# A decoder trunk's head: squares summed by TensorE, nine-column sums for the conditioning, another chain to h, constant products

## The chip, the core and the metric

The kernel runs on one core of a Trainium2 chip. The metric is the device time of one execution in microseconds; the kernel before has a median of 1943.88 (1943.31 to 1947.8 over three runs). Engines have names: TensorE (PE, with its weight loads PEld), VectorE (DVE), ScalarE (ACT), GpSimd (POOL) and SyncE (SP). SyncE and GpSimd issue the DMAs that matter here, each on a queue of its own.

## The reference

One layer of a decoder trunk, for 256 prompt tokens and 8 sequences of 8 sample tokens, 320 tokens in all, of width 2048. Nine conditioning vectors (one of the prompt, eight of the samples) give six modulations of width 2048, and the first two make h:

```
mod = silu(c) @ w_ada + b_ada                      # (9, 6 * 2048)
sh1, sc1, g1, sh2, sc2, g2 = split(mod, 6)
h = rmsnorm(x, norm1_g) * (1 + sc1) + sh1
p = h @ w_in                                       # q, k, v, og, u, ga, gb, alr
o = gated linear attention(q, k, v, alr);  y_b = pooling(u)
x = x + g1 * ((sigmoid(ga) * norm(o) * silu(og) + sigmoid(gb) * y_b) @ w_o)
h2 = rmsnorm(x, norm2_g) * (1 + sc2) + sh2
x = x + g2 * ((silu(h2 @ w_gate) * (h2 @ w_up)) @ w_down)
```

All is fp32. Weights are read once from HBM.

## The kernel before

Activations lie transposed, 128 channels by 320 tokens a tile, 16 tiles for a width of 2048 (KT). A product with fp32 accuracy is made of three fast ones (`mm3`, L177 to L179): the weight is split by ScalarE into a high part (`whi`, L162) and by VectorE into a low part (`wlo`, L163), the activation in the same way (`hh`, `hl`), and low times low is left out. The weights of `w_in` come in by SyncE (`raw`, L218 and L154), three buffers of 512 KB and four of each split part.

**The head** is what the change touches. It makes h while the first group's projections run. The width of h is cut into slices of 2, 2, 2, 2, 4 and 4 tiles; each slice goes through all eleven column blocks ("units") of the first head group, in six groups, and the sums are collected in SBUF. A slice needs its h tiles only, so the conditioning of later tiles runs as background work between the units (`bg`).

Conditioning: for two tiles of h there are two blocks, section 0 (shift) and section 1 (scale), 2 MB of `w_ada` each. `hada_load` brings a block into one of two buffers (tag `araw`); the first two blocks come by SyncE behind `xt`, the others by GpSimd, each as soon as the block two before it has been multiplied. `hada` multiplies it with silu(c) in 16 products, four at a time side by side in the array (L241), which leaves four partial sums of nine rows each, 32 partitions apart. ScalarE copies them to SBUF (`adasb`, L244), TensorE transposes them (L133), VectorE adds the four (L249), then the bias (L252) and for the scale 1 and the norm's weight (L254). The later sections go the same way through `ada_burst` (L306).

h itself: squares by ScalarE (L529), added up to one tile by VectorE (L531 to L533), summed over the channels by one product with ones (L535), root and reciprocal (L537, L538), x times that (`h_pre`, L544), then `h_post`: the affine step (L347 to L349) and the split into `hh` and `hl` (L342, L343).

The order of the work on each engine is made once, when the kernel is built, by a scheduler that goes by priority and by its own idea of times; on the chip every engine takes its list strictly in order, and each SyncE or GpSimd DMA waits in its list too. `high_priority` moves work ahead, `issue_after` forbids it to stand ahead of a given instruction.

Of the kernel before, what the change touches and what calls it, by code (L numbers as in the profile page):

```python
# [11 lines left out]
F32 = mybir.dt.float32  # L12
# [7 lines left out]
P = 128  # L20
# [57 lines left out]
def body(tc, A):  # L78
# [52 lines left out]
    def tr(out, in_):  # L131
        k = in_.shape[0]
        PE.transpose(out, in_, ident[:k, :k])  # L133

    identr = cp.tile([P, P], F32R, name="identr")

    def trr(out, in_):
# [95 lines left out]
    def hada(sec, b0, t, pool):  # L233

        blk = sec * KT + b0
        w = 2 * P
        ps = misc()
        with tc.high_priority():
            for r in (3, 2, 1, 0):
                for j in range(4):  # L240
                    PE.matmul(ps[32 * j:32 * j + 32, 0:w], lhsT=scT[:, 4 * r + j, :], rhs=t[:, 4 * r + j, :],  # L241
                              start=r == 3, stop=r == 0, tile_position=(0, 32 * j))
        sb = pool.tile([P, w], F32, tag="adasb", name=nm("adasb"))
        S.copy(sb, ps[:, 0:w])  # L244
        pt = misc()
        for i in range(2):
            tr(pt[:, i * P:(i + 1) * P], sb[:, i * P:(i + 1) * P])
        dst = mod[:, blk:blk + 2, :]
        V.tensor_reduce(dst, pt[:, 0:w].rearrange("p (b j r) -> p b r j", b=2, j=4)[:, :, 0:9, :],  # L249
                        axis=AX.X, op=ALU.add)  # L250
        bb = bada[:, blk:blk + 2].unsqueeze(2).broadcast_to([P, 2, 9])
        V.tensor_tensor(dst, dst, bb, op=ALU.add)  # L252
        if sec == 1:
            V.scalar_tensor_tensor(dst, dst, 1.0, N1G[:, b0:b0 + 2].unsqueeze(2).broadcast_to([P, 2, 9]),  # L254
                                   op0=ALU.add, op1=ALU.mult)

# [21 lines left out]
    def anchor(src):  # L278

        return G.tensor_copy(tick, src).ins  # L280
# [12 lines left out]
    def ada_burst():  # L293
# [18 lines left out]
        for q in range(0, nb, 2):  # L312
            wq = min(2, nb) * P
            sb = apool[0].tile([P, wq], F32, tag="adasb", name=nm("adasb"))
            S.copy(sb, ps[:, q * P:q * P + wq])
# [3 lines left out]
        V.tensor_reduce(mod[:, blk:blk + nb, :], pt[:, 0:w].rearrange("p (b j r) -> p b r j", b=nb, j=4)[:, :, 0:9, :],  # L319
                        axis=AX.X, op=ALU.add)  # L320
# [20 lines left out]
    def hilo(hi, lo, x):  # L341
        S.copy(hi, x)  # L342
        V.tensor_sub(lo, x, hi.bitcast(F32))  # L343
# [166 lines left out]
    with tc.tile_pool(name="head", bufs=1) as xp:  # L510
# [7 lines left out]
            nc.sync.dma_start(xt[:, k:k + 4], A["xt"][:, k:k + 4])  # L518
        raws = {(s, 0): hada_load(s, 0, xp, nc.sync) for s in (0, 1)}
        make_identity(nc, ident)  # L520
        S.copy(identr, ident)
        csig = xp.tile([P, KT, 9], F32, name="csig")
        S.activation(csig, c9, AF.Sigmoid)
        V.tensor_tensor(scT[:, :, 0:9], c9, csig, op=ALU.mult)

        ssq = xp.tile([P, 4, T], F32, name="ssq")
        for k in range(0, KT, 4):
            sq = xp.tile([P, 4, T], F32, tag="sqx", name=nm("sqx")) if k else ssq
            S.activation(sq, xt[:, k:k + 4], AF.Square)  # L529
            if k:  # L530
                V.tensor_tensor(ssq, ssq, sq, op=ALU.add)  # L531
        V.tensor_tensor(ssq[:, 0:2], ssq[:, 0:2], ssq[:, 2:4], op=ALU.add)
        V.tensor_tensor(ssq[:, 0], ssq[:, 0], ssq[:, 1], op=ALU.add)  # L533
        prs = misc()
        PE.matmul(prs[:, 0:T], lhsT=ones, rhs=ssq[:, 0], start=True, stop=True)  # L535
# [29 lines left out]

        g0 = new_group(0)
        new_gates(g0)
        def h_rows(b):

            def load(s):  # L570
                with tc.issue_after(landed) if (s, b) == (0, 2) else nullcontext():
                    raws[s, b] = hada_load(s, b, xp, nc.gpsimd)
            return ([lambda: load(0), lambda: (h_pre(b), h_pre(b + 1)), lambda: load(1),
                     lambda: hada(0, b, raws.pop((0, b)), xp),
                     lambda: (hada(1, b, raws.pop((1, b)), xp), h_post(b), h_post(b + 1))])

        landed = anchor(raws[0, 0][:, KT - 1, 0:1])
        for f in h_rows(0)[1::2]:
            f()
        with tc.high_priority():  # L580
            h_rows(0)[4]()
        us = [units(0)[0:2], units(0)[4:5], units(0)[2:4]] + [units(0)[n:n + 2] for n in (5, 7, 9)]
        apool = [xp]
        for si, (k0, k1) in enumerate(SLICES):
# [9 lines left out]
                    nc.gpsimd.dma_start(invc, A["cf"][:, 0:64])  # L594
            done = 0
            for ui, pair in enumerate(us):
                want = len(bg) * (ui + 1) // len(us)
                while done < want:
# [562 lines left out]
```

## Time and profile before

| | us |
|---|---|
| median of three runs | 1943.88 |
| the profiled execution | 1946.53 |
| its span, first to last instruction | 1944.8 |
| TensorE busy | 1894.2 (97%) |
| first product of the projections starts at | 29.42 |
| granted clock of TensorE, mean | 0.994 |

The page gives busy time by engine; the timeline gives single instructions in order of time, with the idle time before them and what ended it in brackets. "x2" merges neighbours of one kind, with the time from the first start to the last end. The records of a plain fp32 product come in two passes, those of a transpose and of the fast products in one.

### The profile page before, as it was taken

To read this page: it belongs to the slowest core of one execution; us is meant where nothing else is said; L and a number is where in the kernel's file an instruction comes from. 1 tells how busy PE (TensorE), PEld (TensorE's weight loads), DVE (VectorE), ACT (ScalarE), POOL (GpSimd) and SP (SyncE) were. 2 spreads that over 40 slices of the span, in tenths; PEclk is the share of its full clock that TensorE was granted. 3 is DMA by queue.
4 is the path that set the end of the run, shared out by engine and by line. 5 is a ranking of instruction groups with operands and counts; after the bars stand their busy time and mean duration, and the time that the engine had idled before them with its cause. 6 is when DMAs were issued, how large, how long until landed. Compare 5 with 4: busy or idle time off the path is not lost.

```text
span 1944.8 us, 34340 instructions
## 1 busy us (share of the span) xinstructions
PE 1894.2 (97%) x13698; PEld 1795.0 (92%) x13698; DVE 1019.5 (52%) x1977; ACT 806.4 (41%) x1441; POOL 151.5 (8%) x292
## 2 busy tenths in 40 slices
PE   5999999999999999999999999999999999999996
PEld 4888898988998899889989999999999999999996
DVE  4775564656355646555574444444444444444454
ACT  4333454544354453444453333343333343434442
POOL 1110111121011102101020000000000000000000
PEclk9999999999999999999999999999999999999998
DMA  9996566677766767588644555445554444444542
GB/s 352 365 354 217 194 221 227 210 254 264 247 242 211 262 240 282 192 290 313 208 164 151 185 184 186 143 144 153 146 156 151 149 151 152 152 149 145 153 146 92
DMA packets 102464, 398.54 MB, mean 205 GB/s; under 512 B 12084, under 2 KB 14576, under 8 KB 90008
## 3 DMA queue, kind: packets, MB, share of 16 engines
q1 hardware_dynamic: 77616, 261.73, 42.3%
q0 software_dynamic: 24400, 134.54, 18.0%
q8 instruction: 107, 1.75, 0.4%
q14 instruction: 53, 0.43, 0.1%
q10 hardware_dynamic: 288, 0.08, 0.0%
HBM read 374.48 MB, written 22.05 MB: 204 GB/s over the span
## 4 chain that ended last, share of the span: by engine, by line
PE 87%; DMA 2%; DVE 1%; issue 0%; POOL 0%; ACT 0%; DVEq 0%; POOLq 0%; ACTq 0%
PE ps L177 26%; PE ps L178 26%; PE ps L179 26%; PE pm L306 3%; DMA araw<-w_ada 2%; PE pm L133 1%; PE pm L846 1%; PE pm L808 1%; PE pm L797 0%; DVE yg L1112 0%; PE pm L873 0%; PE pm L651 0%; PE pm L559 0%; DVE S L878 0%; PE pm L745 0%
## 5 line engine op out<-in xcount | busy, mean ns | idle before, releaser
L163 DVE TENSOR_TENSOR wlo<-raw,whi 128x512 fp32r<-128x512 f32 x952 | 660.9, 697 | 764.2 <-ACT whi L162 745.8
L162 ACT CAST whi<-raw 128x512 fp32r<-128x512 f32 x952 | 589.2, 621 | 954.5 <-PE ps L178 888.8
L177 PE MATMUL ps<-hh,whi 128*128 128x320 f32 x1408 | 442.7, 315 | 4.2 <-ACT hh L342 2.9
L179 PE MATMUL ps<-hh,wlo 128*128 128x320 f32 x1408 | 439.3, 312 | 2.3 <-DVE wlo L163 2.3
L178 PE MATMUL ps<-hl,whi 128*128 128x320 f32 x1408 | 440.1, 313 | 0.0
L178 PE MATMUL ps<-h2l,whi 128*128 128x320 f32 x1408 | 435.2, 309 | 0.0
L177 PE MATMUL ps<-h2h,whi 128*128 128x320 f32 x1408 | 435.2, 309 | 0.0
L179 PE MATMUL ps<-h2h,wlo 128*128 128x320 f32 x1408 | 434.7, 309 | 0.0
L177 PEld LDWEIGHTS ps<-hh,whi 128*128 128x128 f32 x1408 | 265.7, 189 | 17.8 <-issue 9.9
L178 PEld LDWEIGHTS ps<-hl,whi 128*128 128x128 f32 x1408 | 265.9, 189 | 9.3 <-issue 8.8
L179 PEld LDWEIGHTS ps<-hh,wlo 128*128 128x128 f32 x1408 | 265.8, 189 | 7.9 <-issue 4.8
L177 PEld LDWEIGHTS ps<-h2h,whi 128*128 128x128 f32 x1408 | 264.5, 188 | 3.4 <-ACT ah L342 3.4
L178 PEld LDWEIGHTS ps<-h2l,whi 128*128 128x128 f32 x1408 | 264.7, 188 | 0.1
L179 PEld LDWEIGHTS ps<-h2h,wlo 128*128 128x128 f32 x1408 | 264.6, 188 | 0.0
L177 PE MATMUL ps<-ah,whi 128*128 128x320 f32 x704 | 217.8, 309 | 0.0
L179 PE MATMUL ps<-ah,wlo 128*128 128x320 f32 x704 | 217.5, 309 | 0.0
L178 PE MATMUL ps<-al,whi 128*128 128x320 f32 x704 | 217.5, 309 | 0.0
L178 PEld LDWEIGHTS ps<-al,whi 128*128 128x128 f32 x704 | 132.3, 188 | 0.1
L177 PEld LDWEIGHTS ps<-ah,whi 128*128 128x128 f32 x704 | 132.3, 188 | 0.1
L179 PEld LDWEIGHTS ps<-ah,wlo 128*128 128x128 f32 x704 | 132.3, 188 | 0.0
L177 PE MATMUL ps<-mh,whi 128*128 128x320 f32 x256 | 79.2, 309 | 0.2 <-DVE mg L505 0.2
L178 PE MATMUL ps<-ml,whi 128*128 128x320 f32 x256 | 79.2, 309 | 0.0
(271 smaller groups left out, 1455.4 us busy)
## 6 DMA issues: line engine op xcount, KB each, us to landing
raw<-w_gu SPq DMA_DIRECT2D x176, 512.0 KB, 3.9
raw<-w_in SPq DMA_DIRECT2D x154, 512.0 KB, 4.6
araw<-w_ada POOLq DMA_DIRECT2D x64, 1024.0 KB, 9.2
raw<-w_down SPq DMA_DIRECT2D x80, 512.0 KB, 3.6
hraw<-w_ada POOLq DMA_DIRECT2D x28, 1024.0 KB, 8.9
S<-state_gla POOLq DMA_DIRECT2D x16, 1024.0 KB, 8.2
o_gs<-S POOLq DMA_DIRECT2D x16, 1024.0 KB, 8.4
raw<-w_o SPq DMA_DIRECT2D x32, 512.0 KB, 5.9
```

The costliest lines, as they stand in the source:

```text
L133: PE.transpose(out, in_, ident[:k, :k])
L162: S.copy(hi, raw)
L163: V.tensor_sub(lo, raw, hi.bitcast(F32))
L177: PE.matmul(ps, lhsT=whi, rhs=xhi, start=start, stop=False)
L178: PE.matmul(ps, lhsT=whi, rhs=xlo, start=False, stop=False)
L179: last_mm[:] = [PE.matmul(ps, lhsT=wlo, rhs=xhi, start=False, stop=stop).ins]
L306: PE.matmul(ps[32 * j:32 * j + 32, 0:w], lhsT=scT[:, k0 + r + j, :], rhs=ada_raw[n][:, r + j, :], start=k0 == 0 and first, stop=k0 + nk == ...
L808: PE.matmul(pt, lhsT=E["kdn"][:, s, d * P:(d + 1) * P], rhs=E["vn"][:, s], start=s == 0, stop=s == 1)
L846: PE.matmul(pt[32 * j:32 * j + 32, :], lhsT=qeP[:, d, 4 * gg + j, :], rhs=E["S0", gg, d][:, j], start=False, stop=d == 0, tile_position=(0 ...
```

## The change

Five things, all but one in the head.

The squares: each quarter of x is squared into a buffer of its own (two of them), VectorE adds its halves, and TensorE sums the two tiles that are left with two products each, eight in all, into one accumulator.

The nine-column sums: in place of two transposes and VectorE's reduction, each half of `adasb` is the stationary operand of a product with `sel`, a 128 by 9 matrix of zeros and ones, which adds the four partial sums and turns them in one. VectorE then adds the bias while it reads the result. This goes for all six sections.

The chain to h: `h_post` is written out. ScalarE makes the high part of the prompt's tokens straight from x, scale and shift; VectorE does the samples, then the same affine step for the low part.

The order: a block's products may no longer stand ahead of the last `mm3` recorded before them, the copies and sums have high priority, and the background work has three steps a row in place of five, dealt out one unit group earlier. The next load of a buffer is recorded right behind the product that frees it; the anchor on the first block's landing (`tick`) is gone.

The constant products: `busy` issues products of ones that nobody reads, two behind the first block's sums and three behind the second's.

```diff
+    sel = cp.tile([P, 9], F32, name="sel")
+    bada1 = cp.tile([P, KT], F32, name="bada1")
...
-        with tc.high_priority():
+        with tc.high_priority(), tc.issue_after(last_mm[0]) if last_mm else nullcontext():
...
-        for i in range(2):
-            tr(pt[:, i * P:(i + 1) * P], sb[:, i * P:(i + 1) * P])
-        dst = mod[:, blk:blk + 2, :]
-        V.tensor_reduce(dst, pt[:, 0:w].rearrange("p (b j r) -> p b r j", b=2, j=4)[:, :, 0:9, :],
-                        axis=AX.X, op=ALU.add)
-        bb = bada[:, blk:blk + 2].unsqueeze(2).broadcast_to([P, 2, 9])
-        V.tensor_tensor(dst, dst, bb, op=ALU.add)
-        if sec == 1:
-            V.scalar_tensor_tensor(dst, dst, 1.0, N1G[:, b0:b0 + 2].unsqueeze(2).broadcast_to([P, 2, 9]),
-                                   op0=ALU.add, op1=ALU.mult)
+        with tc.high_priority():
+            sb = pool.tile([P, w], F32, tag="adasb", name=nm("adasb"))
+            S.copy(sb, ps[:, 0:w])
+            pt = misc()
+            for i in range(2):
+                mm = PE.matmul(pt[:, 16 * i:16 * i + 9], lhsT=sb[:, i * P:(i + 1) * P], rhs=sel, start=True, stop=True)
+            for i in range(2):
+                if sec == 1:
+                    V.tensor_scalar(mod[:, blk + i, :], pt[:, 16 * i:16 * i + 9], bada1[:, b0 + i:b0 + i + 1],
+                                    N1G[:, b0 + i:b0 + i + 1], op0=ALU.add, op1=ALU.mult)
+                else:
+                    V.tensor_scalar(mod[:, blk + i, :], pt[:, 16 * i:16 * i + 9], bada[:, blk + i:blk + i + 1], None,
+                                    op0=ALU.add)
+        return mm.ins
...
-                tr(pt[:, (q + i) * P:(q + i + 1) * P], sb[:, i * P:(i + 1) * P])
+                PE.matmul(pt[:, 16 * (q + i):16 * (q + i) + 9], lhsT=sb[:, i * P:(i + 1) * P], rhs=sel, start=True, stop=True)
...
-        ssq = xp.tile([P, 4, T], F32, name="ssq")
+        prs = misc()
         for k in range(0, KT, 4):
-            sq = xp.tile([P, 4, T], F32, tag="sqx", name=nm("sqx")) if k else ssq
+            sq = xp.tile([P, 4, T], F32, tag="sqx", bufs=2, name=nm("sqx"))
             S.activation(sq, xt[:, k:k + 4], AF.Square)
-            if k:
-                V.tensor_tensor(ssq, ssq, sq, op=ALU.add)
...
-        PE.matmul(prs[:, 0:T], lhsT=ones, rhs=ssq[:, 0], start=True, stop=True)
+            V.tensor_tensor(sq[:, 0:2], sq[:, 0:2], sq[:, 2:4], op=ALU.add)
+            for j in range(2):
+                PE.matmul(prs[:, 0:T], lhsT=ones, rhs=sq[:, j], start=k + j == 0, stop=k + j == KT - 3)
...
         def h_post(k):
+
             xh = xhs.pop(k)
-            affine(xh, 1, 0, k)
-            hilo(hh[k], hl[k], xh)
+            V.tensor_tensor(s3(xh[:, TP:T]), s3(xh[:, TP:T]), mods(1, k), op=ALU.mult)
+            S.activation(hh[k][:, 0:TP], xh[:, 0:TP], AF.Identity, scale=modp(1, k), bias=modp(0, k))
+            V.tensor_tensor(s3(xh[:, TP:T]), s3(xh[:, TP:T]), mods(0, k), op=ALU.add)
+            S.copy(hh[k][:, TP:T], xh[:, TP:T])
+            V.tensor_scalar(xh[:, 0:TP], xh[:, 0:TP], modp(1, k), modp(0, k), op0=ALU.mult, op1=ALU.add)
+            V.tensor_sub(hl[k], xh, hh[k].bitcast(F32))
+
+        def busy(n, after):
+
+            pw = misc()
+            with tc.high_priority(), tc.issue_after(after):
+                for _ in range(n):
+                    PE.matmul(pw[:, 0:2 * P], lhsT=ones, rhs=cst[:, 0:2 * P], start=True, stop=True)
...
-                with tc.issue_after(landed) if (s, b) == (0, 2) else nullcontext():
-                    raws[s, b] = hada_load(s, b, xp, nc.gpsimd)
...
+            def sh():
+                mm = hada(0, b, raws.pop((0, b)), xp)
+                if b + 2 < KT:
+                    load(0, b + 2)
+                return mm
...
-        landed = anchor(raws[0, 0][:, KT - 1, 0:1])
-        for f in h_rows(0)[1::2]:
-            f()
+        r0 = h_rows(0)
+        r0[0]()
+        busy(2, r0[1]())
         with tc.high_priority():
-            h_rows(0)[4]()
+            r0[2]()
...
-                want = len(bg) * (ui + 1) // len(us)
+                want = len(bg) * (ui + 2) // len(us) if ui < 5 else len(bg)
```

**GpSimd, from the head's small fills to the first loads of blocks.** `hraw` is a block of `w_ada`, `tick` the anchor. Before:

```order
masks.py:199 AFFINE_SELECT cst<-cst 128x128
L562 MEMSET alr 32x384
L280 COPY tick<-hraw_137 128x1
L230 DMA hraw_277<-w_ada 128x2048 x2
L230 DMA hraw_345<-w_ada 128x2048 x2
L230 DMA hraw_563<-w_ada 128x2048 x2
```

And now, on the same engine at the same place:

```order
masks.py:199 AFFINE_SELECT cst<-cst 128x128
L575 MEMSET alr 32x384
L232 DMA hraw_212<-w_ada 128x2048 x2
L232 DMA hraw_242<-w_ada 128x2048 x2
L232 DMA hraw_350<-w_ada 128x2048 x2
```

The anchor is gone; the first of these loads follows the first block's products (its buffer), the second the second's.

**TensorE, from the sum of squares to the first product of the projections.** `pm` is a small PSUM tile, `ps` a projection's. Before:

```order
L535 MATMUL pm_164<-ssq,cst 128x320
L241 MATMUL pm_179<-hraw_137,scT 32x256 x16
L133 MATMUL pm_198<-cst,adasb_196 128x128
L241 MATMUL pm_203<-hraw_140,scT 32x256 x16
L133 MATMUL pm_198<-cst,adasb_196 128x128
L133 MATMUL pm_222<-cst,adasb_220 128x128 x2
L177 MATMUL ps_241<-hh_85,whi_242 128x320
```

And now:

```order
L536 MATMUL pm_155<-sqx_156,cst 128x320 x2
L536 MATMUL pm_155<-sqx_161,cst 128x320 x2
L536 MATMUL pm_155<-sqx_166,cst 128x320 x2
L536 MATMUL pm_155<-sqx_171,cst 128x320 x2
L243 MATMUL pm_188<-hraw_139,scT 32x256 x16
L250 MATMUL pm_207<-sel,adasb_205 128x9 x2
L562 MATMUL pm_215<-cst 128x256 x2
L243 MATMUL pm_218<-hraw_142,scT 32x256 x16
L250 MATMUL pm_237<-sel,adasb_235 128x9 x2
L562 MATMUL pm_245<-cst 128x256 x3
```

The first block follows eight products with squares in place of one; each block's sums follow it, with the constant products (L562) behind them.

**ScalarE and VectorE, from the root of the squares to the first h tiles.** `whi` and `wlo` are the parts of a `w_in` load, `adasb` a block's result. ScalarE, before:

```order
L244 COPY adasb_196<-pm_179 128x256
L162 CAST whi_242<-raw_238 128x512
L162 CAST whi_260<-raw_238 128x512
L162 CAST whi_283<-raw_280 128x512
L244 COPY adasb_220<-pm_203 128x256
L162 CAST whi_310<-raw_306 128x512
L342 CAST hh_85<-xh_175 128x320
```

ScalarE now:

```order
L247 COPY adasb_205<-pm_188 128x256
L164 CAST whi_269<-raw_265 128x512
L164 CAST whi_287<-raw_265 128x512
L164 CAST whi_307<-raw_304 128x512
L247 COPY adasb_235<-pm_218 128x256
L164 CAST whi_357<-raw_353 128x512
L551 ACTIVATE hh_87<-xh_184,mod 128x256
```

And VectorE now, up to the samples' first step:

```order
L256 TENSOR_SCALAR mod<-pm_207,bada 128x9 x2
L165 TENSOR_TENSOR wlo_270<-raw_265,whi_269 128x512
L165 TENSOR_TENSOR wlo_288<-raw_265,whi_287 128x512
L165 TENSOR_TENSOR wlo_308<-raw_304,whi_307 128x512
L165 TENSOR_TENSOR wlo_358<-raw_353,whi_357 128x512
L253 TENSOR_SCALAR mod<-pm_237,bada_84,vec 128x9 x2
L550 TENSOR_TENSOR xh_184<-xh_184,mod 128x64
```

As before, three splits of `w_in` loads stand ahead of the second block's copy on ScalarE and a fourth ahead of the first h tile; on VectorE four low parts stand ahead of the scales.

More of the change, by code (lines that the diff above doesn't have):

```diff
@@ L520, in body @@
         make_identity(nc, ident)
+        V.tensor_reduce(sel, ident.rearrange("p (j r) -> p r j", j=4)[:, 0:9, :], axis=AX.X, op=ALU.add)
         S.copy(identr, ident)
+        V.tensor_scalar(bada1, bada[:, KT:2 * KT], 1.0, None, op0=ALU.add)
         csig = xp.tile([P, KT, 9], F32, name="csig")
@@ L596, in body @@
             for ui, pair in enumerate(us):
-                want = len(bg) * (ui + 1) // len(us)
-                while done < want:
+                want = len(bg) * (ui + 2) // len(us) if ui < 5 else len(bg)
+                while done < min(want, len(bg)):
                     bg[done]()
```

24 lines of the change are left out of this document (12 added, 12 removed).

## The prediction

> **What bounds the kernel now.** The page first. Its execution spans 1944.8 us (1946.5 us as a run, against a median of 1943.9), and TensorE is busy in 97% of it:
> ```profile
> span 1944.8 us, 34340 instructions
> PE 1894.2 (97%) x13698; PEld 1795.0 (92%) x13698; DVE 1019.5 (52%) x1977; ACT 806.4 (41%) x1441; POOL 151.5 (8%) x292
> ```
> So a change of the head is worth what it does to TensorE: when the projections begin, at what clock, how long the small products take, where it waits. The table of stretches around the beginning (PE busy, loads, DVE, ACT, POOL, then granted clock, DMA share, GB/s) shows the clock falling to half in the gap before the projections:
> ```profile
> 21.98:25.39 3.41, 2.82 (x46) 1.31 (x38) 3.09 (x7) 1.93 (x4) 1.09 (x2) 1.00 0.72 224
> 25.39:28.81 3.42, 0.63 (x3) 0.20 (x2) 3.09 (x13) 0.89 (x2) 1.05 (x2) 1.00 0.97 401
> 28.81:35.64 6.83, 6.22 (x23) 6.19 (x24) 2.22 (x7) 1.79 (x4) 0.00 (x0) 0.50 1.00 393
> 35.64:39.00 3.36, 3.36 (x43) 2.24 (x42) 1.07 (x2) 1.85 (x4) 0.81 (x2) 1.00 1.00 390
> ```
> 23 products of the first projections ran at half clock. The timeline gives the chain in front of them:
> ```profile
> 5.84 1.27 ACT L529 ACTIVATE ssq<-xt 128x1280 f32<-128x1280 f32 x1 [2.38 <-DMA xt<-xt]
> 10.93 1.27 ACT L529 ACTIVATE sqx<-xt 128x1280 f32<-128x1280 f32 x1 [1.56 <-DVE ssq L531]
> 16.14 0.46 POOL L280 COPY tick<-hraw 128x1 f32<-128x1 f32 x1 [13.28 <-DMA hraw<-w_ada]
> 16.58 0.82 DVE L532 TENSOR_TENSOR ssq<-ssq 128x640 f32<-128x640 f32 x1
> 17.99 1.43 PE L535 MATMUL pm<-ssq,cst 128*128 128x320 f32 x2 [17.99 <-DVE ssq L533]
> 19.35 3.21 PE L241 MATMUL pm<-hraw,scT 128*32 128x256 f32 x32
> 22.91 1.66 ACT L162 CAST whi<-raw 128x512 fp32r<-128x512 f32 x3
> 23.18 1.09 POOL L230 DMA_DIRECT2D hraw<-w_ada  x2 [6.59 <-issue]
> 27.52 0.18 DVE L254 SCALAR_TENSOR_TENSOR mod<-mod,vec 128x18 f32<-128x18 f32 x1
> 29.42 0.90 PE L177 MATMUL ps<-hh,whi 128*128 128x320 f32 x2 [2.89 <-ACT hh L342]
> 35.93 1.93 PE L241 MATMUL pm<-hraw,scT 128*32 128x256 f32 x32
> 38.19 1.05 POOL L230 DMA_DIRECT2D hraw<-w_ada  x2 [11.49 <-PE pm L241]
> ```
> The first conditioning block (L241) starts at 19.35 though its weights had landed by 16.14; it stood behind the sum of squares (17.99). Its end lets GpSimd load the third block, at 23.18.
>
> **The start, step by step.** Squares: each quarter now needs a square, a 640-wide add (0.82, L532) and two products. One product is two records (L535 x2), 1.43 at half clock, so some 0.53 a pass. With two square buffers the quarters end near 10.1, 12.4, 14.6 and, the clock being up by then, 15.8. The first block then starts when its load lands, 16.1, and at full clock ends at 18.1 (1.93, row 35.93): 4.5 us earlier than before. GpSimd issues the next load 0.35 later (37.86 to 38.19).
>
> That is what costs. What was under way on the DMA queues then:
> ```profile
> DMA to landing us min/median/max: 10.2/13.1/15.2
> DMA to landing us min/median/max: 11.0/13.7/15.5
> q1 hardware_dynamic: 721, 1.33, 71.2%
> q0 software_dynamic: 11, 0.09, 11.6%
> ...
> q0 software_dynamic: 395, 2.91, 78.4%
> q1 hardware_dynamic: 357, 0.67, 21.7%
> ```
> The first row is SyncE's four block loads (last issued at 5.84, so landing at 21.0), the second its first five loads of w_in (issued 6.21 to 13.65, so landing 21.7 to 24.65). The next two are 20 to 25 us (packets, MB, share of time): SyncE's queue (q1) alone moved the 1.33 MB of those five loads, and GpSimd's (q0) 0.09 MB, so its bytes start about 1.4 us after the issue at 23.18. The last two are 28 to 37 us, both queues pending: about as many packets of each, but 2.91 MB on GpSimd's and 0.67 MB on SyncE's, 323 and 74 GB/s. A GpSimd load thus starves w_in.
>
> Before, the five loads were through when the third block's load began. Now its bytes begin at 18.1 + 0.35 + 1.4 = 19.9, ahead of all five. The second block runs at about 21.5 to 23.4 and lets the fourth block's load follow at 25.2, so GpSimd has 4.2 MB pending without a break: 4.2/0.323 = 13.0 us, to 32.9. SyncE finishes the second block near 21.4 and then moves a w_in load of 0.262 MB in 3.5 us: 24.9, 28.4, 31.9, and the fourth, the queue free again, at 33.4.
>
> ScalarE and VectorE are strictly in order, and the rows show what stands behind: the copy of the second block's sums behind the third load's split, the scales (L253) behind the fourth's. From 33.4: split 0.62, low part 0.7, scales 0.4, then 1.2 to h (before, 27.52 to 29.42 took 1.9 with one longer chain): first product at **36.3** against 29.42. Where before the first 24 products were through by 35.93, they now end at 36.3 + 24 x 0.145 + 0.2 = 40.0: **+4.1**. The fillers cover little: two follow the first block, and the three of the second wait for its sums, near 32. The clock is lost while TensorE idles from 23.4; with the three at half clock (2.6 us) it is back at once or three microseconds late, +0 to +1.3; I take **+0.6**. Bounds of the start: -6.2 if nothing starves (second rival), +7.5 if the fifth load and the clock are both late.
>
> By the Trainium skill ("TensorE: Matmul & The Clock Gate", Part 1) the gate looks at free-running windows of about 3.4 us and drops after an idle one. This trace agrees in kind (changes at 21.98, 28.81, 35.64, two windows apart); by that rule three fillers may or may not fill a window, so the sum could lose the 0.6 or double it.
>
> **The nine-column sums.** 96 transposes go. What a pair costs, and what weight loads cost where the product is short:
> ```profile
> L133 PE MATMUL pm<-cst,adasb 128*128 128x128 f32 x96 | 18.7, 275 | 1.8 <-ACT adasb L244 1.1 <-ACT adasb L315 0.7
> ...
> 145.95 0.31 PE L178 MATMUL ps<-hl,whi 128*128 128x320 f32 x1
> ...
> 146.10 0.31 PE L179 MATMUL ps<-hh,wlo 128*128 128x320 f32 x1
> ...
> 146.25 0.38 PE L133 MATMUL pm<-cst,adasb 128*128 128x128 f32 x2
> ...
> 146.38 0.39 PE L177 MATMUL ps<-hh,whi 128*128 128x320 f32 x1
> ...
> 146.61 0.31 PE L178 MATMUL ps<-hl,whi 128*128 128x320 f32 x1
> ...
> 259.86 0.41 PEld L678 LDWEIGHTS pm<-cumr,w 128*128 128x128 f32 x3
> ...
> 270.48 0.97 PEld L820 LDWEIGHTS pm<-qeP,keP 128*128 128x128 f32 x8
> ...
> 369.26 0.81 PEld L139 LDWEIGHTS pm<-identr,vTP 128*128 128x128 f32 x8
> ```
> Products of the stream follow at 0.145. The L178 after a pair of transposes should stand at 146.39 and stands at 146.61: a pair costs 0.22, 0.11 for each single pass. The data stay the stationary operand in the new form, 128 columns, and a plain fp32 product takes two passes (L535, x2), each with its load. So 92 transposes after the start become 184 passes. The load does not shrink with nine columns: 0.11 apart at L678 ((0.41 - 0.19)/2) and L820 ((0.97 - 0.19)/7), 0.096 at L139 in transpose mode ((0.81 - 0.14)/7). At 0.11 a pair costs 0.44, 0.22 more, or +10.1 for 46 pairs; at 0.087 (L139 with its first gap taken as a whole product's 0.145) +5.9. No row has a nine-column product, so the lower bound is a pass that follows as fast as half a transpose, +0, or faster still, -2. I take 0.10, between L139 and the two that load in the same way as the sums: 0.40 a pair, 0.18 more, **+8.3**.
>
> VectorE's part gets cheaper (two reads of nine columns for a reduce and two adds); at 52% busy it is worth nothing but the latency counted above.
>
> **Waits later.** TensorE's waits in the head after the start, with what stood in front of them on ScalarE, and the page's price of a low part:
> ```profile
> PE ps L179 <- DVE wlo L163: 2.3, 2, 1.2
> PE ps L177 <- ACT whi L162: 0.3, 1, 0.3
> ...
> 158.37 0.82 ACT L342 CAST hh<-xh 128x320 fp32r<-128x320 f32 x2 [5.64 <-DVE xh L349]
> ...
> L163 DVE TENSOR_TENSOR wlo<-raw,whi 128x512 fp32r<-128x512 f32 x952 | 660.9, 697 | 764.2 <-ACT whi L162 745.8
> ```
> ScalarE stood 5.64 us on the last h pair with weight splits queued behind it. In the new order that pair's sums come over 40 products ahead of need: **-2.0** of the 2.6 (bounds 0 and -2.6). Against it: at slices two to four the second block's sums stand 26 products (3.8 us) ahead of the slice's first, and VectorE needs some 4.2 from sums to low part, since an evacuation and two weight splits (0.7 each) stand between the small steps: 0.3 for each slice, **+1.0** (0 to +2.5). The later block loads do not starve: they come later by product count, and 2.1 MB at 323 GB/s is 6.5 us against 9 to 14 between blocks. The other ScalarE pieces of the chain to h are hidden by its 41%.
>
> Sum: 4.1 + 0.6 + 8.3 - 2.0 + 1.0 = **+12.0** on the span, so 1958.5 for a run like the profiled one and a median of **1956**.
>
> **Rivals.**
> *The sums cost no more than the transposes.* For: nine columns stream in no time. Against: L678 above. 4.1 + 0.6 - 2.0 + 1.0 = +3.7: 1947.6.
> The Trainium skill (same page, "Architectural detail") says that a product may begin before its weights are all loaded. If so, passes close up, and this rival holds; no row here shows it for 128 fp32 columns.
>
> *The start gains in full, the sums cost.* If w_in keeps its rate beside GpSimd's load, the second block ends at 23.0 and h follows 3.2 later (4.1 before): first product 26.2, 24 of them by 29.7 at full clock, -6.2. With 8.3 - 2.0 + 1.0: +1.1, 1945.0. Against it, the 28 to 37 us rows. A partial form: a first block at half clock ends at 20.2, two w_in loads get through, and the first product comes near 31.5, about level with before.
>
> *Faster: the queue decides it alone.* Place: the five w_in loads between 20 and 33 us. If they land by 26, the start gives -6.2, the vanished stall -2.0, and the change is faster as soon as a pair of sums costs under 0.05 us more than its transposes: -8.2, 1935.7. For it: the loads lost by 28 to 37 were issued after GpSimd's, while these stand in SyncE's queue ahead; an engine may serve what it has already taken.
>
> *The change does not do what it says:* the fillers sit where TensorE would have been busy or warm anyway. The forecast has it so already for three of the five, and for the other two it would change nothing: 1956.
>
> **How the numbers follow.** Forecast 0.50, since three rows have the loads of 128 columns near 0.1 and two the shared queues; sums free 0.17; start gains and sums cost 0.15; both, faster, 0.18. This kernel's measurement tells about 0.3% (5.8 us) from no change. The two middle rivals fall within it: same 0.32. The forecast is slower: 0.50; the last faster: 0.18. The forecast's own range is 1951 (no clock loss, sums +5.9, the stall gone in full, nothing at the slices: +7.4) to 1962 (start +7.5, sums +10.1, slices +2.5, stall -2.0: +18.1); with the faster rival taken in it is 1935 to 1962.
>
> **What would show it.** Right: GpSimd's block load issued near 18.5, the first product after 33 us with ScalarE's split waiting on w_in in front of it, half clock between about 28 and 35, and weight loads of the sums 0.11 apart, four to a pair. Wrong: splits of w_in by 25 us and a first product near 26 at full clock; or four passes in 0.25 us. If the time falls below 1940, the first product has come early and the sums are cheap.

## The result, and the profile after

The changed kernel takes 1954.57 us (median of four runs, 1953.42 to 1959.18) against 1943.6 for the kernel before in the same runs: a ratio of 1.0054, 95% interval 1.0039 to 1.0069, or 11.0 us more. The forecast was 1956, slower. The profiled execution (1959.18 us) is the longest of the four; one event in it, named below, explains part of that. Its page begins:

```profile
span 1957.4 us, 34586 instructions
PE 1914.5 (98%) x13818; PEld 1811.8 (93%) x13818; DVE 1014.5 (52%) x1970; ACT 812.2 (41%) x1457; POOL 152.4 (8%) x291
```

TensorE's share went from 97% to 98%, and the kernel got slower: it is busier with small products.

Where the time went shows best when both traces are laid beside each other by progress. Both issue the same 11,424 fast products of the projections, so the n-th in one trace can be set against the n-th in the other ("done" is its start and one step of the stream, 0.147 us). Between the 24th and the 792nd the two place blocks of the conditioning at different counts; at the 792nd both have done all sixteen.

| product | before, us | after, us | lag |
|---|---|---|---|
| first starts | 29.42 | 30.58 | +1.2 |
| 24th done | 35.83 | 36.60 | +0.8 |
| 792nd done | 183.81 | 186.79 | +3.0 |
| 3100th done | 629.11 | 636.43 | +7.3 |
| last starts | 1926.38 | 1939.04 | +12.7 |

A quarter of the loss arises in the head, the rest in the four sections after it, where of the code only the nine-column sums changed; 1.7 us of that rest is an event of this one execution (below).

**The start.** Timeline of the changed kernel, GpSimd, ScalarE and TensorE (columns as in the prediction):

```profile
18.36 1.09 POOL L232 DMA_DIRECT2D hraw<-w_ada  x2 [15.50 <-PE pm L243]
24.65 0.62 ACT L164 CAST whi<-raw 128x512 fp32r<-128x512 f32 x1 [1.55 <-DMA raw<-w_in]
25.17 0.37 ACT L247 COPY adasb<-pm 128x256 f32<-128x256 f32 x1
27.73 0.62 ACT L164 CAST whi<-raw 128x512 fp32r<-128x512 f32 x1 [2.19 <-DMA raw<-w_in]
25.59 1.02 PE L250 MATMUL pm<-sel,adasb 128*128 128x9 f32 x4 [2.58 <-ACT adasb L247]
30.58 0.90 PE L179 MATMUL ps<-hh,whi 128*128 128x320 f32 x2 [1.21 <-ACT hh L553]
```

GpSimd's block load goes out at 18.36, 4.8 us earlier than before. ScalarE then waits twice for `w_in`: its third split starts at 24.65 and the fourth at 27.73, and the copy of the second block's sums stands between them. TensorE idles 2.58 us in front of those sums. The stretches (PE busy, loads, DVE, ACT, POOL, granted clock, DMA share, GB/s) show what that does to the clock:

```profile
21.00:25.45 4.45, 1.93 (x32) 0.94 (x32) 1.54 (x3) 2.04 (x4) 1.05 (x2) 1.00 1.05 407
25.45:28.50 3.05, 2.91 (x9) 2.55 (x10) 0.66 (x2) 0.70 (x2) 0.00 (x0) 0.50 1.03 422
28.50:30.50 2.00, 0.87 (x3) 0.15 (x1) 1.92 (x9) 1.19 (x4) 0.00 (x0) 0.50 0.99 410
30.50:35.70 5.20, 5.12 (x18) 4.90 (x19) 1.95 (x5) 0.18 (x2) 0.00 (x0) 0.50 1.00 409
35.70:39.00 3.30, 2.82 (x19) 2.56 (x18) 0.69 (x1) 1.82 (x3) 0.00 (x0) 1.00 0.30 89
```

Half clock from 25.45 to 35.70, the three constant products behind the second sums included. It lasts 10 us in place of 7, but of the projections only 18 products fall into it, 23 before.

The transfers of the changed kernel, from 18 to 22.3 and from 22.3 to 34 us (packets, MB, share of 16 engines; q0 is GpSimd's queue, q1 SyncE's):

```profile
q1 hardware_dynamic: 557, 1.67, 99.4%
q0 software_dynamic: 9, 0.07, 4.0%
...
q0 software_dynamic: 520, 3.87, 78.5%
q1 hardware_dynamic: 532, 0.97, 22.4%
```

Though issued at 18.36, GpSimd's load moves almost nothing until 22.3. Then the two queues alternate, 520 packets against 532, and SyncE is left with 0.97 MB in 11.7 us, 83 GB/s. Two of the five `w_in` loads got through around that time (21.65 and 22.45 us); the others landed at 24.62, 27.71 and 30.83. Before, all five had landed by 24.65.

**The sums.** One pair in the stream, products and then loads of the changed kernel:

```profile
152.72 0.30 PE L179 MATMUL ps<-hh,whi 128*128 128x320 f32 x1
152.86 0.51 PE L250 MATMUL pm<-sel,adasb 128*128 128x9 f32 x4
153.22 0.39 PE L180 MATMUL ps<-hl,whi 128*128 128x320 f32 x1
153.46 0.31 PE L181 MATMUL ps<-hh,wlo 128*128 128x320 f32 x1
...
152.72 0.55 PEld L250 LDWEIGHTS pm<-sel,adasb 128*128 128x128 f32 x4
```

From L179 to L181 are 0.74 us; without the pair it would be two steps of 0.147. The pair costs 0.45. The same reckoning over all pairs that stand between two fast products gives a median of 0.449 (37 pairs), and 0.220 for the transposes of the kernel before (36 pairs). Four loads stand (0.55 - 0.19)/3 = 0.12 apart here, and the starts of the passes 0.112 apart from the second on (the first load ran beside the product in front of it); nothing closes up behind nine columns.

**The waits.** TensorE's waits between 40 and 200 us, changed kernel:

```profile
PE ps L180 <- DVE hl L555: 0.5, 1, 0.5
PE pm L243 <- DMA hraw<-w_ada: 0.3, 1, 0.3
```

The 2.6 us of waits for weights that the prediction quoted are gone.

**One event.** Late in the run TensorE awaits a block load, and the clock falls for one period of 3.4 us behind the gap (timeline, then stretches):

```profile
848.54 3.36 PE L309 MATMUL pm<-araw,scT 128*32 128x256 f32 x32 [2.58 <-DMA araw<-w_ada]
```

```profile
846.00:848.06 2.06, 0.00 (x0) 1.00 0.85 342
848.06:851.48 3.42, 2.94 (x28) 0.50 0.59 178
```

That costs this execution 1.7 us (half of 3.4). The kernel before waits for a load at that place too (1.76 us, at 839.00), and its clock holds. The traces of these kernels have such periods at different places, and the four executions of the changed kernel rank by them: a mean granted clock of 0.992, 0.993, 0.995 and 0.995 with 1959.18, 1954.80, 1954.35 and 1953.42 us.

### The profile page after: what moved, and what is told of

Same layout as the page of the kernel before. It is cut to its first block, busy times and chain, and to the rows that moved or that the text cites. A ratio compares the mean times of both kernels' runs of the same rounds, so it can differ in the third digit from the quotient of the medians.

```text
span 1957.4 us, 34586 instructions
## 1 busy us (share of the span) xinstructions
PE 1914.5 (98%) x13818; PEld 1811.8 (93%) x13818; DVE 1014.5 (52%) x1970; ACT 812.2 (41%) x1457; POOL 152.4 (8%) x291
## 3 DMA queue, kind: packets, MB, share of 16 engines
q0 software_dynamic: 24400, 134.54, 18.1%
## 4 chain that ended last, share of the span: by engine, by line
PE 92%; DMA 4%; DVE 2%; issue 1%; ACT 0%; POOL 0%; SPq 0%; DVEq 0%; ACTq 0%; POOLq 0%
PE ps L179 28%; PE ps L180 28%; PE ps L181 28%; PE pm L309 3%; DMA araw<-w_ada 1%; PE pm L243 1%; DMA raw<-w_in 1%; PE pm L871 1%; DMA hraw<-w_ada 1%; PE pm L133 1%; PE pm L320 1%; DMA o_gp<-sf 0%; PE pm L833 0%; DMA xt<-xt 0%; DMA S<-state_gla 0%
## 5 line engine op out<-in xcount | busy, mean ns | idle before, releaser
L179 PE MATMUL ps<-hh,whi 128*128 128x320 f32 x1408 | 443.0, 315 | 3.5 <-DVE mg L507 1.8
L181 PE MATMUL ps<-hh,wlo 128*128 128x320 f32 x1408 | 438.3, 311 | 0.0
L179 PE MATMUL ps<-h2h,whi 128*128 128x320 f32 x1408 | 435.1, 309 | 0.0
L181 PE MATMUL ps<-h2h,wlo 128*128 128x320 f32 x1408 | 434.7, 309 | 0.0
L179 PEld LDWEIGHTS ps<-hh,whi 128*128 128x128 f32 x1408 | 265.4, 189 | 21.1 <-issue 13.4
L180 PEld LDWEIGHTS ps<-hl,whi 128*128 128x128 f32 x1408 | 265.5, 189 | 10.2 <-issue 8.5
L181 PEld LDWEIGHTS ps<-hh,wlo 128*128 128x128 f32 x1408 | 265.5, 189 | 2.9 <-issue 2.5
L179 PEld LDWEIGHTS ps<-h2h,whi 128*128 128x128 f32 x1408 | 264.4, 188 | 3.4 <-ACT ah L344 3.4
L181 PEld LDWEIGHTS ps<-h2h,wlo 128*128 128x128 f32 x1408 | 264.4, 188 | 0.0
L179 PE MATMUL ps<-ah,whi 128*128 128x320 f32 x704 | 217.4, 309 | 0.0
L181 PE MATMUL ps<-ah,wlo 128*128 128x320 f32 x704 | 217.2, 309 | 0.0
L179 PEld LDWEIGHTS ps<-ah,whi 128*128 128x128 f32 x704 | 132.2, 188 | 0.1
L181 PEld LDWEIGHTS ps<-ah,wlo 128*128 128x128 f32 x704 | 132.2, 188 | 0.0
L179 PE MATMUL ps<-mh,whi 128*128 128x320 f32 x256 | 79.2, 309 | 0.2 <-DVE mg L507 0.2
```

The source lines that it names most:

```text
L179: PE.matmul(ps, lhsT=whi, rhs=xhi, start=start, stop=False)
L180: PE.matmul(ps, lhsT=whi, rhs=xlo, start=False, stop=False)
L181: last_mm[:] = [PE.matmul(ps, lhsT=wlo, rhs=xhi, start=False, stop=stop).ins]
```

## The experiments

All ratios are against the kernel before, run on the same chip in the same set, with their 95% intervals; the changed kernel stands at 1.0054 (1.0039 to 1.0069).

### The sums alone

The kernel before with only this:

```diff
...
-            tr(pt[:, i * P:(i + 1) * P], sb[:, i * P:(i + 1) * P])
+            PE.matmul(pt[:, 16 * i:16 * i + 9], lhsT=sb[:, i * P:(i + 1) * P], rhs=sel, start=True, stop=True)
...
```

(in `hada` and `ada_burst`; VectorE copies nine columns in place of its reduction).

> The kernel before with the nine-column sums alone, in all six sections. Theory (0.23 us a pair on the stream): the kernel before plus 10.6, about 1954.2. Rival (the sums cost nothing where they stand): within 2 us of the kernel before, 1943.6. If it comes out between, the price of a pair depends on what stands around it.

Measured: 1.0051 (1.0039 to 1.0064), 9.9 us. A pair costs 0.448 in its trace. One edit of the five is as slow as all of them together. In this trace the lag is 0.7 us at the 792nd product and 8.0 at the last.

### The sums taken back

The changed kernel with transposes, a reduction and the bias added apart, in all sections:

> The changed kernel with the conditioning's nine-column sums put back to two transposes and a reduction, in all six sections; order, squares, chain to h and constant products stay. Theory (each pair of sums costs 0.45 us of TensorE's stream and each pair of transposes 0.22, so 46 pairs cost 10.6 us more): the changed kernel minus 10.6, about 1944, and a lag behind the kernel before that no longer grows after the head. Rival (the sums are free, and the loss comes from the new order of the background work and the start): within 2 us of the changed kernel, about 1954.

Measured: 1.0026 (1.0015 to 1.0038), 5 us over the kernel before, between the two theories. A pair of transposes costs 0.223 here, so the price is right. From the 792nd product to the end, too, the lag no longer grows, as expected: this trace gains 1.8 us on the kernel before where the changed one loses 9.7. (The 1.8 are the clock's: the kernel before has a period of 3.4 us at half clock from 291.63 on, worth 1.7, and this trace has none.) But at the 792nd it stands 4.3 us behind, although 14 pairs are cheaper by 3.2. So the sums alone cost 9.9 us and the other four edits without them 5, but all five only 11. New waits have come, between 40 and 200 us:

```profile
PE ps L179 <- ACT hh L554: 1.3, 2, 0.8
PE ps L180 <- DVE hl L556: 0.9, 2, 0.6
PE pm L243 <- DMA hraw<-w_ada: 0.6, 1, 0.6
PE ps L179 <- DVE mg L402: 0.5, 1, 0.5
PE ps L179 <- DVE q L402: 0.4, 2, 0.2
```

TensorE waits for h at the start of the second and the third slice, where the spacing of its products exceeds 0.147 by 1.7 and 2.5 us in three gaps each. VectorE's timeline of this kernel in front of the first of these waits (58.12) tells why, and beside it the same place of the changed kernel:

```profile
53.81 0.23 DVE L252 TENSOR_REDUCE mod<-pm 128x18 f32<-128x72 f32 x1 [0.48 <-PE pm L250]
54.11 0.82 DVE L406 TENSOR_SCALAR mg<-ps 128x640 f32<-128x640 f32 x1
54.85 0.17 DVE L255 TENSOR_TENSOR mod<-mod,bada 128x18 f32<-128x18 f32 x1
54.94 0.68 DVE L165 TENSOR_TENSOR wlo<-raw,whi 128x512 fp32r<-128x512 f32 x1
55.54 0.17 DVE L257 TENSOR_TENSOR mod<-mod,vec 128x18 f32<-128x18 f32 x1
```

```profile
54.50 0.48 DVE L253 TENSOR_SCALAR mod<-pm,bada,vec 128x9 f32<-128x9 f32 x2 [0.61 <-PE pm L250]
```

With transposes the scale takes three small steps, and the order puts an evacuation (0.82) and a weight's low part (0.68) between them: 1.9 us from TensorE's result to the scale. With the sums it is one instruction, twice, 0.48. The forecast had called that "worth nothing but the latency counted above".

### Transposes only after the head

> The changed kernel with transposes put back only in the four sections after the head (32 pairs); the head is the changed one. Theory: 32 x 0.226 = 7.2 us less than the changed kernel, which stood at a ratio of 1.0054, so a ratio near 1.0017, and the lag behind the kernel before stays near 3 us from the end of the head on. Rival (the lag after the head comes from clock drops and later block loads, not from the sums): the lag still grows to over 8 us, a ratio over 1.004.

Measured: 1.0020 (1.0011 to 1.0030), where 1.0017 was expected. The lag is 3.4 us at the 792nd product and 1.1 at the end. From there to the end this trace gains 2.3 where the changed kernel loses 9.7. Of these 12.0 us the sums are 7.2 (32 pairs at 0.226) and 3.4 are two clock periods (295 and 848 us) that the changed kernel's trace has and this one has not; 1.4 are not placed. So the loss after the head is mainly the sums'.

### Sixty-four columns in place of nine

```diff
-    sel = cp.tile([P, 9], F32, name="sel")
+    sel = cp.tile([P, 64], F32, name="sel")
...
```

> The changed kernel with the moving matrix of the sums widened from 9 to 64 columns (the rest zeros), in all six sections. Theory (a pass costs its load of 128 columns, 0.112 us, whatever is streamed behind it): passes 0.112 us apart as before, a pair 0.45 us, no change of the time beyond 1 us. Rival (a pass costs by its moving columns plus a fixed part): passes further apart, a pair over 0.5 us and over 2 us more in the run.

```profile
76.65 0.31 PE L179 MATMUL ps<-hh,whi 128*128 128x320 f32 x1
76.80 0.56 PE L250 MATMUL pm<-sel,adasb 128*128 128x64 f32 x4
77.16 0.39 PE L180 MATMUL ps<-hl,whi 128*128 128x320 f32 x1
77.39 0.31 PE L181 MATMUL ps<-hh,wlo 128*128 128x320 f32 x1
```

Again 0.74 from L179 to L181; the median over 37 pairs is 0.447. Seven times the columns cost a pair nothing: with both widths a pass costs the 0.112 at which the loads of 128 stationary columns follow each other. The single run, 1959.65 us, can't tell 1 us from the changed kernel's 1953 to 1959, and an event falls into it, a wait for another load with half clock behind it (426.06 to 432.88, 3.4 us):

```profile
427.97 3.64 PE L872 MATMUL pm<-S,qeP 128*32 128x512 f32 x16 [3.83 <-DMA S<-state_gla]
```

### The early loads held back

The changed kernel, but GpSimd's third and fourth block load wait for the fifth `w_in` load ("the gated kernel" below):

```diff
...
+                raw = raw_pair(win, [u[2] for u in pair], k0, 2) if k1 - k0 == 2 else [None] * 2
+                if si == 0 and ui == 2:
+                    gate[:] = [anchor(raw[1][:, 1, 255:256])]
+                    with tc.issue_after(gate[0]):
+                        load(0, 2)
+                        load(1, 2)
...
```

> The changed kernel, but GpSimd's loads of the third and fourth block wait until the fifth early load of w_in has landed; the third block's products stand 12 products later. Theory (the early block loads starve the fourth and fifth w_in load, which land at 27.7 and 30.8 us in the changed kernel): they land by 24.7, the first projection product comes near 27.3 in place of 30.6, and the run is 2 to 3 us shorter, about 1952. Rival (w_in is not what the first product waits for, or the clock gate takes the gain back with more products at half clock): first product earlier or not, but less than 1 us gained, about 1954.

Measured: 1.0038 (1.0026 to 1.0051), some 3 us less than the changed kernel's ratio; the two intervals overlap, but the trace is plain. The five loads land by 24.54, the first product starts at 26.99, 3.6 earlier, and the 24th is done at 31.15, 5.5 earlier, because the clock does not fall there (PE busy, granted clock, DMA share, GB/s):

```profile
21.00:24.50 3.50, 2.15 (x34) 1.00 0.79 301
24.50:27.00 2.50, 1.80 (x11) 1.00 0.74 197
27.00:31.00 4.00, 3.73 (x23) 1.00 0.98 356
```

### The constant products, with and without the gate

The gated kernel without the five:

> The gated kernel with sums everywhere, without the five constant products; the order of ScalarE at the start is held. Theory (with the gate the first product came at 27.0 and TensorE kept its full clock, and the constant products at 19.5 and 24.8 are what kept it there): without them TensorE idles from 24.9 to 27, the clock falls to half for 3.4 or 6.8 us around the first products, and the 24th product comes 1.5 to 3 us later than with them. Rival (the constant products are too short to matter, 2.7 us of work in 9): the clock and the first 24 products as with them, within 0.3 us.

```profile
21.00:24.50 3.50, 2.13 (x34) 1.00 0.72 269
24.50:27.00 2.50, 0.42 (x4) 0.91 0.72 206
27.00:31.00 4.00, 3.99 (x14) 0.50 0.95 297
```

The first product stands at 27.01 as with them, but the clock is at half until 33.38, and the 24th is done at 33.60, 2.4 us later. As timed, 1.0037 (1.0024 to 1.0050), it is not told from the gated kernel; five and four runs with a spread of 3 us do not resolve 2.

The changed kernel, without the gate, without the five:

> The changed kernel without the five constant products; the order of ScalarE at the start is held. Theory (in the changed kernel TensorE idles 2.6 us before the second block's sums, which costs the clock anyway, so the constant products do nothing there): half clock at the first projection products as with them, the 24th product within 0.7 us of the changed kernel's 37.2. Rival (the three behind the sums bring the clock back sooner): the clock stays at half 3.4 us longer and the 24th product comes 1 us or more later.

One run, 1955.02 us. Without them the clock is at half for as long, 10.2 us, but in two parts, from 21.72 to 25.13 and from 28.55 to 35.37, and the 24th product is done at 35.71, 0.9 us *earlier* than with them. (The 37.2 of the expectation is the start of the 25th; by the same measure the changed kernel has 36.60.) That misses the numbers of both theories. But in this execution the third `w_in` load landed at 23.67 in place of 24.62 and the fourth at 26.35 in place of 27.71, so one trace of each doesn't show what the constant products did here.

How far the five loads get ahead of GpSimd's bytes differs between traces: in the six whose GpSimd load goes out between 18.4 and 18.7 us (the changed kernel and five of these runs), the third lands between 23.15 and 25.32 and the first product starts between 29.17 and 31.29. So fillers pay when they bridge the whole gap (gated), and did not hold the clock where an idle stretch of 2.6 us remained.

### The squares as before

> The changed kernel with the squares summed as before (three full adds and two halvings by VectorE, one product); the order of ScalarE at the start is held as in the changed kernel. Theory (finishing the first block early is what costs: it lets GpSimd's loads start 5 us earlier, among the w_in loads): with the first block at 19.4 again, GpSimd's load issues at 23, the five w_in loads land by 24.7, and the first product comes at 28.5 to 29.5, earlier than the 30.6 of the changed kernel, by 1 to 2 us in the run. Rival (an earlier first block is worth what it saves): the first product comes later, at 32 or more, and the run is 2 to 4 us longer than the changed kernel.

Measured: 1.0038 (1.0025 to 1.0051). The first product starts at 30.11, only 0.5 us earlier, which misses the 28.5 to 29.5 expected. Two constant products now stood ahead of the second block's products and among them (from 23.16 and 24.32, 0.7 us each), which would account for it. But the loads land by 24.60, the clock holds, and the 24th is done at 34.16, 2.4 us earlier than with the faster squares. In these two traces, finishing the first block later made the start faster; the ratio is lower too, but the two intervals overlap.

### The chain to h as before

> The changed kernel with the chain to h as before (two steps of VectorE over the whole tile, one rounding by ScalarE, one subtraction). Theory (the chain matters only where TensorE waits for h: at the first product and at the first products of the second and third slice): the first product 0.3 to 0.8 us later than the changed kernel's 30.6, the waits at the starts of slices together up to 2 us longer, the run 0.5 to 2.5 us longer, a ratio of 1.0057 to 1.0067. Rival (ScalarE's extra pieces delay the weight splits as much as VectorE gains): no difference in the waits.

Measured: 1.0062 (1.0049 to 1.0076). The first product starts at 31.02, 0.4 later. Since that start moves by 2 us between traces with the landing of the fourth `w_in` load, the time from this landing is the better measure: 3.35 us here, 2.87 in the changed kernel, 2.87 to 2.98 in the four other traces with the new chain. The waits between fast products in the head, read off their spacing (with the 0.1 that follows each small product), are some 5.0 us against 4.1. Both are as expected; the difference of the ratios is within the intervals, so as a time it is not shown.

### Put together

Transposes everywhere and the gate:

> Both edits together: transposes in place of the nine-column sums, and GpSimd's third and fourth block loads held back until the early w_in loads have landed. Theory (the two losses add up, and what is left of the change gains): the changed kernel minus 10.6 minus 2.5, about 1941.5, some 2 us under the kernel before. Rival (what is left of the change is worth nothing or costs): 1943.6 or more.

Measured: 1.0002 (0.9994 to 1.0011). 2.6 us ahead at the first product, 1.2 behind at the 792nd: the waits of the second and third slice again, and in this execution the clock fell behind them, at 83.0.

The gate, sums for the first three pairs of blocks, transposes elsewhere (`if b0 > 4` in `hada`):

> The changed kernel with GpSimd's third and fourth block load held back until the early w_in loads have landed, nine-column sums kept for the first three pairs of blocks only (tiles 0 to 5 of shift and scale), and transposes for all later blocks and sections. Theory (a pair of sums costs TensorE 0.23 us more than its transposes, but in the second and third slice the longer chain of VectorE behind transposes stalls TensorE by 2.5 to 4 us, so sums pay exactly there): against the gated kernel with sums everywhere (its profile ended 5.9 us behind the kernel before) 42 pairs are cheaper by 0.226, -9.5, so 3 to 4 us ahead of the kernel before, a ratio near 0.998. Rival (the stalls of the transposed version come from its order, not from VectorE's chain, and return here): equal to the kernel with transposes everywhere, a ratio of 1.000.

Measured: 0.9982 (0.9974 to 0.9991), 1941.47 us against 1944.88: faster than both kernels by an interval that excludes no change. Its waits between 40 and 200 us:

```profile
PE ps L180 <- DVE hl L568: 0.5, 1, 0.5
PE pm L243 <- DMA hraw<-w_ada: 0.5, 1, 0.5
```

It stands 3.2 us ahead at the 792nd product and 4.9 at the last.

Transposes everywhere, the gate, and more lead:

```diff
-                want = len(bg) * (ui + 2) // len(us) if ui < 5 else len(bg)
+                want = len(bg) * (ui + 2 + (si > 0)) // len(us) if ui < 5 else len(bg)
```

> The kernel with transposes everywhere and the gated loads, but from the second slice on the background work is dealt out one unit group earlier, so that the second block of the third slice is multiplied 72 products ahead of need in place of 48 (the block for the second slice stays at 48). Theory (the stalls of the transposed version are latency behind transposes: VectorE's chain from sums to h is longer than the products in front of it): the stall at the start of the third slice, 2.5 us with transposes in three gaps, falls under 0.5 us, the one at the start of the second slice, 1.7 us, stays, and the run is 2 us shorter than the same kernel without the extra lead (ratio 1.0002), a ratio near 0.999. Rival (the stalls are VectorE throughput, or the load of the weights): the stall at the third slice stays and the ratio too.

Measured: 0.9999 (0.9990 to 1.0007). The stall at the third slice falls from 2.5 us to 0.7 (the sum of what its gaps exceed 0.147), a little over the 0.5 expected, and the one at the second stays at 1.7: latency, as the theory has it. But the run gains almost nothing, since two waits of 1.2 appear near 170 and 179:

```profile
PE ps L181 <- DVE wlo L165: 2.4, 2, 1.2
...
179.07 0.82 DVE L402 SCALAR_TENSOR_TENSOR mg<-ps,mg 128x640 f32<-128x640 f32 x1 [2.40 <-PE ps L181]
179.81 2.49 DVE L165 TENSOR_TENSOR wlo<-raw,whi 128x512 fp32r<-128x512 f32 x4
```

VectorE sat 2.40 us at the head of its list on an evacuation that waited for TensorE, with four low parts behind it, and then TensorE waited for these.

## Why the prediction was right, and which steps were not

The time (1956 forecast, 1954.57 measured) and its sign were right, and the largest term carries the result. The start, the sums and the waits were each mis-sized, and 3.3 us stand in no term of the forecast; that they made up for each other is luck. The table accounts for the profiled execution, the slowest of the four; the medians differ by 11.0.

| term | forecast | profiled execution |
|---|---|---|
| start | +4.1 | +0.8 (24 products done 36.60 against 35.83), clock included |
| cold clock | +0.6 | in the line above |
| evacuation of q at 37 us | none | +0.5 |
| sums, 46 pairs | +8.3 | +10.5 (0.229 each) |
| stalls gone and new ones in the head | -2.0 + 1.0 | -1.95 (3.07 to 1.12) |
| clock period at 848 | none | +1.7 |
| sum | +12.0 | +11.6, with 1.1 not placed: +12.7 |

*The sums.* "I take 0.10, between L139 and the two that load in the same way" was the step that missed: the loads are 0.112 apart, which L678 and L820 had shown, and the bound worked out from them (+10.1) was the answer. L139 is a transpose, a pass of its own kind, and had no claim on the middle. That each plain product is two passes of load was right, and the whole result hangs on it. The rival by the Trainium skill ("TensorE: Matmul & The Clock Gate", "Architectural detail"), that a product may begin before its weights are loaded, does not shorten a pass here: in the records the products do start while their loads still run (153.002 against a load from 152.974 to 153.165), but the passes close up no further than the loads, and with 9 and with 64 columns they stand 0.112 apart. The Trainium skill ("TensorE: Matmul & The Clock Gate", "LDWEIGHTS") prices a load by its columns, P/1.2 ns; the estimate of 107 ns for 128 columns is near the 112 measured. And the Trainium skill ("Perfetto Trace Analysis", section "Transposes") says to use the transpose and not a standard product for a transposition; this case's 0.22 against 0.45 us a pair bears it out, though the products here also add.

*The start.* The chain was right: the block load at 18.36 (18.5 forecast), packets taken in turns, SyncE at 83 GB/s (74 forecast), 3.1 us for a starved `w_in` load (27.71 to 30.83; 3.5 forecast), ScalarE's split waiting in front of h, and 2.87 us from the fourth load's landing to the first product (0.62 + 0.7 + 0.4 + 1.2 = 2.92 forecast). The step that failed is "its bytes start about 1.4 us after the issue", so "its bytes begin at 18.1 + 0.35 + 1.4 = 19.9, ahead of all five". They began at 22.2, 3.8 us after the issue, when one `w_in` load had landed and the second was nearly through. So the fourth landed at 27.71 and not at 33.4, and the first product came at 30.58 and not at 36.3; the sign named for it, a first product after 33 us, did not come. This is the form that the prediction mentioned and set aside: two loads "get through, and the first product comes near 31.5, about level with before". The rival's sentence "an engine may serve what it has already taken" fits the delay, but no run isolates it.

*The clock.* Half clock from 25.45 to 35.70 against "between about 28 and 35". With 18 products of the projections in it, where there were 23, it costs no more than before, and the +0.6 was not there. That the three fillers could not hold it was right for this kernel; the gated one shows where they can.

*The waits.* The -2.0 was right, by a wrong reading in part. The last of the three gaps in the kernel before (the product at 169.92) was put down to ScalarE's 5.64 us at the last h pair, ten microseconds earlier. VectorE's timeline of the kernel before has another cause:

```profile
168.44 0.82 DVE L399 SCALAR_TENSOR_TENSOR og<-ps,og 128x640 f32<-128x640 f32 x1 [2.40 <-PE ps L179]
169.18 2.48 DVE L163 TENSOR_TENSOR wlo<-raw,whi 128x512 fp32r<-128x512 f32 x4
```

It is the form that came back with the extra lead: an evacuation at the head of VectorE's list with four low parts behind it. New waits at slices two to four were foreseen at 0.3 each; two were measured, 0.2 and 0.9.

*VectorE.* "...at 52% busy it is worth nothing but the latency counted above": too little. Where the list leaves 26 products between sums and need, the shorter chain is worth 3 us in the second and third slice, and there the sums earn back what TensorE pays. Nothing in the prediction asked what transposes would do in the *new* order.

## What to carry to other kernels

Price a small product by its loads and its passes, not by its columns: here a transpose was one pass of 0.11 us and a plain fp32 product two, so replacing transposes by products doubled the cost on an engine that had no gap left, and the shorter VectorE chain paid only where h was waited for within a few microseconds. Before freeing a buffer earlier, ask which transfers its next load will meet: a queue with large packets (7.4 KB on average, against 1.8) took four fifths of the bandwidth from loads that were needed first, and holding it back by 6.8 us (18.36 to 25.12) finished the first 24 products 5.5 us earlier. The same edit can cost in one place and pay in another (the sums cost 9.9 us alone and everywhere, and paid in six pairs of 48), so try the pieces of a change apart and by place.

## What the runs showed of the hardware that was not expected

GpSimd's load, issued while SyncE still had 2.7 us of a block and all five `w_in` loads ahead, moved its first bytes 3.8 us after the issue (18.36 to 22.2; 3.8 to 3.9 in the traces of five more kernels with the same start), against 1.3 us in the kernel before (23.18 to 24.45), with two loads and the end of a third ahead. Once it flowed, the queues soon alternated (39 packets of SyncE's and 37 of GpSimd's between 23 and 24 us). So what is already queued ahead is partly safe and partly not, and the boundary moves: the third of the five loads landed between 23.15 and 25.32 in these six traces. The Trainium skill ("DMA: Bandwidth & Descriptors", "Queues, rings and completion order") has an engine take turns between queues by packets; from 22.3 us on the trace agrees, as the profile counts packets (520 against 532), while the first 3.8 us are not explained by it.

The clock can be held through 9 us of thin work by 2.7 us of constant products (gate, with them: full clock from 12.99 to 1934.7 us; without them: half from 26.55 to 33.38). In the changed kernel, where an idle stretch of 2.58 us lies between them, the same five did not hold it (half from 25.45).
